# A short-convolution and latent-attention block: the attention and the first part of its output projection put into the hand-written instruction list, and weight parts moved from GpSimd to VectorE

## The chip, the cores and the metric

The kernel runs on one core of a Trainium2 chip. The metric is the device time in microseconds (us). The engines are named as the profile names them: PE is TensorE (matmuls and transposes), DVE is VectorE, ACT is ScalarE, POOL is GpSimd, SP is SyncE, which here only issues DMAs.

## The reference, cut to what matters

One convolution layer and one attention layer, each followed by a gated feed-forward part, on 1024 tokens of width 1024, with 8 heads. All arithmetic is float32. The part that the change touches:

```python
k_nope, v = kv[..., :128], kv[..., 128:]          # kv = c_lat @ w_ukv, per head
q = (cq @ w_uq).reshape(b, s, 8, 128 + 64)
q_pe = apply_rope(q[..., 128:], cos_h, sin_h)     # the last 64 of each head are rotated
# for each block of 128 queries:
sc = einsum('bqhd,bkhd->bhqk', qn_b, k_nope) + einsum('bqhr,bkr->bhqk', qr_b, k_pe)
p = softmax(where(mask, sc * scale, neg))         # causal mask
o = einsum('bhqk,bkhd->bqhd', p, v)
h = h + attn.reshape(b, s, 8 * 128) @ w_o         # the output projection
```

## The kernel before, in words

**Products.** A float32 product is made of three matmuls in the type float32r: each operand is held as a high part and a low part (what is left), and high*high, high*low and low*high are summed. `split` makes the parts: ACT copies to the high part (line 111), then DVE, or another engine if told, subtracts it from the source (line 112). `gemm` (lines 146 to 150) and `three` (lines 153 to 155) issue the matmuls. Activations lie with features on the partitions and 1024 tokens along the free dimension.

**The order of the work.** Most stages are written as one list, a `Steps` object. Each step holds a piece of PE work; functions can be hung before or after a step, to load something, to make parts or to empty a PSUM bank. `run` emits all this in a region in which every engine keeps the order of emission. A step number smaller by two means: emitted two PE pieces earlier. The attention is not such a list. Its functions are called one after the other, and the framework's scheduler sets the order on each engine by its own estimate of time.

**The attention before.** `steps.run()` ends the list of the stages ahead (feed-forward of the first layer, latent products, and the K, Q and V of head 0 and K of head 1, in `ahead`). Then a loop runs over the 8 heads. In each, `scores` (line 1438 its matmuls) makes eight blocks of 128 queries against 128 to 1024 keys: five products, the mask by a minimum (1439), the maximum (1441), its scaling (1442), the exponential with its row sum on ACT (1445), the reciprocal (1446) and the scaling of the block on DVE (1447). `pv` transposes the blocks by PE (1460, tile `ps_t`), splits them (tile `pt`) and multiplies with the values (1469 to 1471, tile `ps_pv`), with the product two key blocks behind the transposes. `pv` for the first four query blocks (g = 0) comes in the same head, for the last four (g = 1) in the next one. Between them stand the jobs that make K, Q, V and the rotated part of Q for the next heads (`make_k`, `make_q`, `make_v`, `make_qr`). Their weights are loaded and split by `Weights.all`, which gives the low part to POOL. `make_qr` also adds and splits on POOL. During head 7 the jobs are `project_o`, the output projection's share of heads 0 to 4 for the eight output blocks; its weights' low parts are on POOL too (`wsplit`). Heads 0 to 5 are stored in DRAM (`od`) and read back, heads 6 and 7 stay in SBUF.

**What comes after.** A second `Steps` list begins with `Plain`, the projection's share of heads 5 to 7 (tile `pl`), whose weights are loaded and split by `wo_load` and `wo_parts`; then the norm and the feed-forward of the second layer.

**Buffers.** PSUM in the attention (`ATT_PS`) has two double banks (tag `ps2`: wide scores, K, Q, V, projection) and four single banks (tag `ps1`: narrow scores, transposes, `ps_pv`). The weights' raw data share five buffers, the parts of the weights four.

## Time and profile before

| | us |
|---|---|
| median of 3 runs (lowest, highest) | 2126.71 (2124.61, 2128.39) |
| the profiled execution | 2122.53 |
| its span, first to last instruction | 2120.6 |
| first scores' matmul, last start of one | 1096.7, 1389.2 |

The profiled execution lies 4.2 us below the median, and 1.9 us of it lie outside the span. In the rows of groups, the name before the arrow is the tile written, those behind it are read; after x stands the count, then the busy time and the mean of one in ns, then the idle time of the engine before them and what ended it. A row of the waits names who waited, what for, the sum in us, how often and the longest. A row of windows gives for each engine its busy time in that stretch and in brackets its instructions, then the granted clock of PE (1.00 is full), the share of the DMA engines and their rate. Matmuls overlap, so the duration of one is longer than the distance to the next.

### The profile page before, as it was taken

How to read it: one execution, taken by the hardware profiler on the slowest of the kernel's cores; microseconds unless marked ns; L12 is line 12 of the kernel's file. 1: busy time of each engine (PE TensorE's matmuls, PEld its weight loads, DVE VectorE, ACT ScalarE, POOL GpSimd, SP SyncE). 2: the span in 40 equal slices, each digit the busy share in tenths (PEclk: the TensorE clock that was granted, in tenths of full speed). 3: DMA queues.
4: the chain of work that ended last, by engine and by line, in shares of the span. 5: the costliest groups of instructions: out<-in, count | busy, mean ns of one | idle time of the engine just before them, and what ended most of it. 6: DMA issues, size and time to landing. Idle time of an engine off the chain costs nothing.

```text
span 2120.6 us, 25572 instructions
## 1 busy us (share of the span) xinstructions
PE 2066.0 (97%) x9542; PEld 1706.4 (80%) x9542; DVE 1460.6 (69%) x2175; ACT 858.0 (40%) x1439; POOL 315.2 (15%) x412
## 2 busy tenths in 40 slices
PE   7999999999999999999999999989999999999998
PEld 6778888888888887787888888877888888888777
DVE  5787656887666668867577777437886666667555
ACT  7423434433333333354245555225433333333445
POOL 2233200122122210000023232101111111100000
PEclk9999999999999999999999999999999999999999
DMA  7255775586766586564232223325487475685543
GB/s 231 70 120 121 226 269 178 117 204 188 186 165 153 139 286 230 193 226 146 70 69 69 65 63 121 138 79 174 128 200 178 149 169 154 154 322 193 179 148 120
DMA packets 274315, 338.96 MB, mean 160 GB/s; under 512 B 18047, under 2 KB 177984, under 8 KB 273872
## 3 DMA queue, kind: packets, MB, share of 16 engines
q1 hardware_dynamic: 240144, 262.71, 38.1%
q0 software_dynamic: 33888, 74.56, 16.4%
q8 instruction: 74, 1.21, 0.2%
q14 instruction: 49, 0.40, 0.1%
q10 hardware_dynamic: 160, 0.07, 0.0%
HBM read 260.22 MB, written 126.35 MB: 182 GB/s over the span
## 4 chain that ended last, share of the span: by engine, by line
PE 83%; DVE 7%; DMA 4%; ACT 3%; issue 2%; SPq 0%; POOL 0%; DVEq 0%; ACTq 0%; POOLq 0%
PE q L154 16%; PE q L153 16%; PE q L155 16%; PE dn L155 4%; PE dn L154 4%; PE dn L153 4%; PE ps_s L1438 4%; PE pl L155 2%; PE pl L153 2%; PE pl L154 2%; DVE wp_lo L112 1%; PE ps_t L1460 1%; PE ps_l L155 1%; PE ps_l L153 1%; PE ps_l L154 1%
## 5 line engine op out<-in xcount | busy, mean ns | idle before, releaser
L153 PE MATMUL q<-xh,w_hi 128*128 128x512 f32 x1568 | 613.3, 391 | 6.3 <-ACT w_hi L111 2.6
L154 PE MATMUL q<-xl,w_hi 128*128 128x512 f32 x1568 | 611.5, 390 | 2.9 <-DVE xl L317 2.9
L155 PE MATMUL q<-xh,w_lo 128*128 128x512 f32 x1568 | 611.5, 390 | 0.9 <-DVE w_lo L112 0.9
L153 PEld LDWEIGHTS q<-xh,w_hi 128*128 128x128 f32 x1568 | 294.8, 188 | 70.6 <-ACT w_hi L111 3.8
L154 PEld LDWEIGHTS q<-xl,w_hi 128*128 128x128 f32 x1568 | 294.7, 188 | 65.9 <-DVE xl L317 4.8
L155 PEld LDWEIGHTS q<-xh,w_lo 128*128 128x128 f32 x1568 | 294.7, 188 | 63.2 <-DVE w_lo L112 2.4
L112 DVE TENSOR_TENSOR w_lo<-wr,w_hi 128x512 fp32r<-128x512 f32 (+1 forms) x272 | 196.6, 723 | 215.1 <-ACT w_hi L111 214.2
L111 ACT CAST w_hi<-wr 128x512 fp32r<-128x512 f32 (+1 forms) x272 | 170.1, 630 | 372.1 <-DVE wr L390 151.2
L155 PE MATMUL dn<-mp_hi,wp_lo 128*128 128x512 f32 (+1 forms) x628 | 245.3, 391 | 6.3 <-DVE wp_lo L112 4.5
L153 PE MATMUL dn<-mp_hi,wp_hi 128*128 128x512 f32 (+1 forms) x628 | 244.3, 389 | 1.0 <-ACT wp_hi L111 1.0
L154 PE MATMUL dn<-mp_lo,wp_hi 128*128 128x512 f32 (+1 forms) x628 | 243.3, 387 | 0.9 <-DVE mp_lo L112 0.9
L1050 POOL COPY paced<-pace 128x1 f32<-128x1 f32 x128 | 84.8, 663 | 923.0 <-ACT pace L1049 923.0
L112 DVE TENSOR_TENSOR mp_lo<-m,mp_hi 128x1024 fp32r<-128x1024 f32 x84 | 95.3, 1134 | 127.2 <-ACT mp_hi L111 125.6
L111 ACT CAST mp_hi<-m 128x1024 fp32r<-128x1024 f32 x84 | 82.2, 979 | 209.8 <-PE dn L154 204.0
L155 PEld LDWEIGHTS dn<-mp_hi,wp_lo 128*128 128x128 f32 x628 | 118.3, 188 | 38.8 <-DVE wp_lo L112 15.5
L153 PEld LDWEIGHTS dn<-mp_hi,wp_hi 128*128 128x128 f32 x628 | 118.3, 188 | 25.5 <-ACT wp_hi L111 2.8
L154 PEld LDWEIGHTS dn<-mp_lo,wp_hi 128*128 128x128 f32 x628 | 118.4, 188 | 25.5 <-DVE mp_lo L112 1.3
L112 DVE TENSOR_TENSOR wp_lo<-w,wp_hi 128x1024 fp32r<-128x1024 f32 x84 | 94.8, 1128 | 0.0
L111 ACT CAST wp_hi<-w 128x1024 fp32r<-128x1024 f32 x84 | 82.0, 976 | 0.0
L1445 ACT ACTIVATE p<-ps_s,mx,rq 128x128 f32<-128x128 f32 (+3 forms) x64 | 53.3, 834 | 56.6 <-DVE mx L1442 51.4
L382 DVE TENSOR_TENSOR w_lo<-wr,w_hi 128x1024 fp32r<-128x1024 f32 x56 | 68.7, 1226 | 7.6 <-ACT w_hi L378 7.6
L738 DVE TENSOR_TENSOR h<-h,dn 128x512 f32<-128x512 f32 x108 | 68.7, 679 | 0.0
(292 smaller groups left out, 3218.8 us busy)
## 6 DMA issues: line engine op xcount, KB each, us to landing
m<-md_f SPq DMA_DIRECT2D x70, 512.0 KB, 4.9
md_f<-c SPq DMA_DIRECT2D x110, 256.0 KB, 3.4
wr<-in_conv_ffn_w_dram SPq DMA_DIRECT2D x47, 512.0 KB, 5.7
wr<-in_mla_ffn_w_dram SPq DMA_DIRECT2D x47, 512.0 KB, 5.4
w<-mw_f SPq DMA_DIRECT2D x40, 512.0 KB, 3.9
h<-hd SPq DMA_DIRECT2D x32, 512.0 KB, 9.3
wr<-in_conv_w_in_dram SPq DMA_DIRECT2D x31, 512.0 KB, 5.2
mw_f<-in_conv_ffn_w_dram POOLq DMA_DIRECT2D x30, 512.0 KB, 7.2
```

What stands on the lines that cost most here:

```text
L111: nc.scalar.copy(out=hi, in_=src)
L112: (eng or nc.vector).tensor_tensor(lo, src, hi.bitcast(F32), ALU.subtract)
L153: nc.tensor.matmul(ps, lhsT=wh, rhs=xh, start=st, stop=False, **more)
L154: nc.tensor.matmul(ps, lhsT=wh, rhs=xl, start=False, stop=False, **more)
L155: nc.tensor.matmul(ps, lhsT=wl, rhs=xh, start=False, stop=en, **more)
L382: nc.vector.tensor_tensor(lo, self.ra, hi.bitcast(F32), ALU.subtract)
L738: nc.vector.tensor_tensor(hv, hv, banks[q], ALU.add if sign > 0 else ALU.subtract)
L1050: nc.gpsimd.tensor_copy(b, a)
L1438: nc.tensor.matmul(ps[:, a:b], lhsT=q[:, qs], rhs=k[:, a:b], start=i == 0, stop=i == 4)
L1445: nc.scalar.activation(p[:, :kw], ps[:, :kw], AF.Exp, bias=mx, scale=rq[:, qb:qb + 1], accum_out=rsum)
L1460: nc.tensor.transpose(t[:, j * P:(j + 1) * P], ps_[j][:, kb * P:(kb + 1) * P], ident)
```

## The change

The attention and the shares of heads 0 to 4 of the projection become steps of the same list as the stages ahead and behind; `steps.run()` between them goes, and with it the second `Steps()`. So every engine takes their instructions in the order written. `scores`, `pv` and `make_qr` are cut into pieces for this. The products stay the same.

- The order of a head: S is the product of one query block (S0 to S7), P the ten or six pieces of `pv`. Odd heads (1, 3, 5): S0 S1 S2 S3, rotated Q, four pieces of the head before's g = 1, Q, the other six, S4 S5, three pieces of g = 0, K, one piece, S6, two pieces, first half of V, S7. Even heads (2, 4, 6): S0 to S3, second half of V, Q, all ten late pieces, S4 S5, three pieces, K, one piece, S6, two pieces, S7. Head 0 has Q for head 1 after S3 and no K; head 7 has output blocks 0, 1 and 2 in the places of the jobs, then 3, 4, five late pieces, 5, five late pieces, 6, 7.
- A block's scaling (reciprocal and scaling) is emitted two steps after its product. For query blocks 4 to 7 the scaling is done by ACT instead of DVE.
- The weights of K, Q and V are loaded nine steps ahead and split four steps ahead, those of the projection six and two; the low parts are made by DVE instead of POOL.
- The rotated part of Q for heads 2 to 7 is made by two ACT copies with the halves of the partitions exchanged, two multiplications 1024 wide, an addition and a split, all on ACT and DVE, spread over seven steps. For the second multiplication a tile `nsin` is loaded (two more DMAs, once).
- `wo_load` and `wo_parts` for heads 5 to 7 stand six steps and one step ahead of `Plain`.

```diff
+        rot["nsin"] = pslot("nsin", "nsin", 1)
+        for q in range(2):
+            nc.sync.dma_start(rot["nsin"][q * 64:q * 64 + 64], rd[1, 64 - q * 64:128 - q * 64])
...
-        def all(self):
-            self.load()
-            return self.split(nc.gpsimd, lo_tile)
...
+    def qr_pieces(h, w):
+        b = {}
+        def product():
+            b["ps"] = q_product(w())
+            b["t"], b["qr"] = tmp("rt"), tmp("qr")
+        def turned(q):
+            nc.scalar.copy(out=b["t"][q * 64:q * 64 + 64], in_=b["ps"][64 - q * 64:128 - q * 64])
+        def cos():
+            nc.vector.tensor_tensor(b["qr"], b["ps"], rot["cos"], ALU.mult)
+        def sin():
+            nc.vector.tensor_tensor(b["t"], b["t"], rot["nsin"], ALU.mult)
+        def add():
+            nc.vector.tensor_tensor(b["qr"], b["qr"], b["t"], ALU.add)
+        def parts():
+            yh, yl = tmp("qrh", dt=F32R), tmp("qrl", dt=F32R)
+            split(yh, yl, b["qr"])
+            qr_moves(h, yh, yl)
+        return product, lambda: turned(0), cos, lambda: turned(1), sin, add, parts
...
+        def scale():
+            p, rsum = Ps[h, qb]
+            nc.vector.reciprocal(rsum, rsum)
+            if qb < 4:
+                nc.vector.tensor_scalar(p[:, :kw], p[:, :kw], rsum, None, ALU.mult)
+            else:
+                nc.scalar.activation(p[:, :kw], p[:, :kw], AF.Copy, scale=rsum)
...
-    steps.run()
...
+    def project_load(n):
+        wo_w[n] = Weights("wo", w_o[:, 0:5, n * P:(n + 1) * P], [P, 5, P])
+        wo_w[n].load()
+        st.h[n] = slot("h")
+        nc.sync.dma_start(st.h[n], hd[n])
...
+    def a_scores(h, *qbs):
+        for qb in qbs:
+            product, scale = scores(h, qb)
+            m = steps.add(product)
+            steps.before(m + 2, scale)
+    def a_job(w, fn):
+        box = {}
+        m = steps.add(lambda: fn(box["w"]))
+        steps.before(m - 9, w.load)
+        steps.before(m - 4, lambda: box.update(w=w.split(new_hi=lo_tile)))
+        return m, box
+    def a_project(n):
+        m = steps.add(lambda: project_o(n))
+        steps.before(m - 6, lambda: project_load(n))
+        steps.before(m - 2, lambda: wo_w.update({n: wo_w[n].split(new_hi=lo_tile)}))
+    def a_rotated(h):
...
+        steps.before(m - 9, w.load)
+        steps.before(m - 4, lambda: box.update(w=w.split(new_hi=lo_tile)))
+        for j, fn in zip((0, 0, 2, 4, 5, 6), pieces):
+            steps.after(m + j, fn)
...
+    for h in range(H):
+        p0 = pv(h, 0)
+        a_scores(h, 0, 1, 2, 3)
+        if h == 7:
+            steps.before(len(steps.pe), lambda: O1.extend([load_o(5, r_(), r_())]))
+            a_project(0)
+            a_steps(late)
+        elif h == 0:
+            a_job(W_q(1), lambda w: make_q(1, w))
+        elif h % 2:
+            a_rotated(h + 1)
+            a_steps(late[:4])
+            a_job(W_q(h + 1), lambda w, h=h: make_q(h + 1, w))
+            a_steps(late[4:])
         else:
+            steps.add(lambda h=h, vbox=vbox: make_v(h, vbox["w"], 1))
+            a_job(W_q(h + 1), lambda w, h=h: make_q(h + 1, w))
+            a_steps(late)
+        a_scores(h, 4, 5)
+        a_steps(p0[:3])
+        if h == 7:
+            a_project(1)
+        elif h:
+            m, _ = a_job(W_k(h + 1), lambda w, h=h: make_k(h + 1, w))
...
+        a_steps(p0[3:4])
+        a_scores(h, 6)
+        a_steps(p0[4:])
+        if h == 7:
+            a_project(2)
+        elif h % 2:
+            _, vbox = a_job(W_v(h + 1), lambda w, h=h: make_v(h + 1, w, 0))
+        a_scores(h, 7)
+        late = pv(h, 1)
+    a_project(3)
+    a_project(4)
+    a_steps(late[:5])
+    a_project(5)
+    a_steps(late[5:])
+    a_project(6)
+    a_project(7)
+    n0 = len(steps.pe)
+    for j, k in enumerate((5, 6, 7)):
+        steps.before(n0 - 6 + j, lambda k=k: wo_load(k))
+        steps.before(n0 - 1 + j, lambda k=k: wo_parts(k))
```

## The prediction

> **What bounds the kernel now.** I read the page first (the engines' shares, then the chain that ended last by engine), then the windows of the attention, then the list of PE's waits there.

> ```profile
> PE 2066.0 (97%) x9542; PEld 1706.4 (80%) x9542; DVE 1460.6 (69%) x2175; ACT 858.0 (40%) x1439; POOL 315.2 (15%) x412
> ...
> PE 83%; DVE 7%; DMA 4%; ACT 3%; issue 2%; SPq 0%; POOL 0%; DVEq 0%; ACTq 0%; POOLq 0%
> ```

> The reader is to see that PE is busy for nearly the whole span and carries the chain. The edit leaves every matmul in place, none more and none fewer. So only PE's waits can move, and in the main only in the stretch that the edit reorders: the heads, from 1080 to 1420 us.

> ```profile
> core 0: us, PE busy (x) PEld busy (x) DVE busy (x) ACT busy (x) POOL busy (x), PEclk, DMA share, GB/s
> 1080.00:1335.00 255.00, 244.32 (x1422) 213.23 (x1421) 193.75 (x458) 132.05 (x274) 72.29 (x101) 1.00 0.31 89
> 1335.00:1420.00 85.00, 77.84 (x367) 64.31 (x364) 31.46 (x49) 20.09 (x35) 9.40 (x6) 0.96 0.27 90
> 1391.40:1394.81 3.41, 0.56 (x4) 0.25 (x2) 3.14 (x4) 1.33 (x2) 0.00 (x0) 1.00 0.91 333
> 1394.81:1401.64 6.83, 6.23 (x15) 4.88 (x16) 2.72 (x5) 1.29 (x2) 0.00 (x0) 0.50 0.70 212
> ...
> PE ps_wo L146 <- DVE h L1521: 3.5, 1, 3.5
> PE ps_s L1438 <- ACT p L1445: 3.4, 2, 2.6
> ```

> PE idles 10.7 us (255.00 - 244.32) in heads 0 to 6 and 7.2 us at the end. There the two long waits leave a window of 3.41 us with 0.56 of PE work, and the next 6.83 us run at clock 0.50, which loses 3.4 more. In all 21.3 us: what an order that never lets PE wait would give back. DVE has 61 us free in the first window and ACT 123, so neither is full; what counts is how long a chain across DVE and ACT is against the PE work put beside it.

> **What is removed, added, moved.** PE's prices, from the timeline:

> ```profile
> 1202.75 0.60 PE L1460 MATMUL ps_t<-ident,p 128*128 128x128 f32 x4
> 1207.58 0.27 PE L1460 MATMUL ps_t<-ident,p 128*128 128x128 f32 x1
> 1208.17 0.63 PE L148 MATMUL ps_k<-lat_part,wk_hi 128*128 128x512 f32 x2
> 1208.64 0.62 PE L150 MATMUL ps_k<-lat_part,wk_lo 128*128 128x512 f32 x2
> ```

> A transpose takes (0.60 - 0.27)/3 = 0.11 us, a 512-column matmul 0.47/2 = 0.23; narrower ones I scale by columns. DVE, then ACT, by shape:

> ```profile
> L112 DVE TENSOR_TENSOR pt<-ps_t,pt 128x512 fp32r<-128x512 f32 x48 | 31.9, 681 | 7.8 <-ACT pt L111 7.7
> L112 DVE TENSOR_TENSOR pt<-ps_t,pt 128x384 fp32r<-128x384 f32 x16 | 8.8, 550 | 0.5 <-ACT pt L111 0.5
> L112 DVE TENSOR_TENSOR pt<-ps_t,pt 128x128 fp32r<-128x128 f32 x16 | 4.5, 283 | 7.2 <-ACT pt L111 7.2
> L112 DVE TENSOR_TENSOR qnl<-ps_q,qnh 128x1024 fp32r<-128x1024 f32 x7 | 8.6, 1222 | 14.0 <-ACT qnh L111 14.0
> L1439 DVE TENSOR_TENSOR ps_s<-ps_s,cmask 128x128 f32<-128x128 f32 x64 | 18.2, 293 | 23.7 <-PE ps_s L1438 23.1
> L1442 DVE TENSOR_SCALAR mx<-mx,nrq 128x1 f32<-128x1 f32 x64 | 12.5, 202 | 0.2
> L1446 DVE RECIPROCAL rsum<-rsum 128x1 f32<-128x1 f32 x64 | 10.0, 156 | 12.3 <-ACT p L1445 12.1
> L1441 DVE TENSOR_REDUCE mx<-ps_s 128x1 f32<-128x1024 f32 x8 | 9.8, 1223 | 0.2
> L1441 DVE TENSOR_REDUCE mx<-ps_s 128x1 f32<-128x896 f32 x8 | 8.7, 1092 | 0.2
> L1441 DVE TENSOR_REDUCE mx<-ps_s 128x1 f32<-128x768 f32 x8 | 7.6, 953 | 0.1
> L1441 DVE TENSOR_REDUCE mx<-ps_s 128x1 f32<-128x512 f32 x8 | 5.5, 685 | 0.0
> L1441 DVE TENSOR_REDUCE mx<-ps_s 128x1 f32<-128x128 f32 x8 | 2.3, 281 | 0.0
> L1447 DVE TENSOR_SCALAR p<-p,rsum 128x1024 f32<-128x1024 f32 x8 | 6.0, 749 | 0.2
> L1447 DVE TENSOR_SCALAR p<-p,rsum 128x512 f32<-128x512 f32 x8 | 4.5, 556 | 0.1
> L1447 DVE TENSOR_SCALAR p<-p,rsum 128x128 f32<-128x128 f32 x8 | 2.2, 278 | 0.1
> ...
> L111 ACT CAST pt<-ps_t 128x512 fp32r<-128x512 f32 x48 | 27.3, 594 | 30.9 <-PE ps_t L1460 29.5 <-DVE mx L1441 1.0
> L1445 ACT ACTIVATE p<-ps_s,mx,rq 128x1024 f32<-128x1024 f32 x8 | 9.7, 1208 | 11.5 <-DVE mx L1442 7.8 <-PE ps_s L1438 3.7
> L1445 ACT ACTIVATE p<-ps_s,mx,rq 128x896 f32<-128x896 f32 x8 | 8.8, 1099 | 18.6 <-DVE mx L1442 18.6
> L1445 ACT ACTIVATE p<-ps_s,mx,rq 128x768 f32<-128x768 f32 x8 | 8.0, 1000 | 1.2 <-DVE mx L1442 1.2
> L111 ACT CAST qnh<-ps_q 128x1024 fp32r<-128x1024 f32 x7 | 7.1, 1010 | 0.0
> L111 ACT CAST wo_hi<-wo_raw 128x640 fp32r<-128x640 f32 x8 | 5.8, 729 | 32.8 <-PE ps_wo L148 20.2 <-issue 12.4 <-DMA wo_raw<-in_mla_w_o_dram 0.2
> L111 ACT CAST wqn_hi<-wqn_raw 128x384 fp32r<-128x384 f32 x6 | 3.1, 519 | 5.2 <-issue 5.1
> ...
> L112 POOL TENSOR_TENSOR wo_lo<-wo_raw,wo_hi 128x640 fp32r<-128x640 f32 x8 | 12.5, 1567 | 65.0 <-ACT wo_hi L111 63.6 <-PE ps_s L1438 1.4
> wo_raw<-in_mla_w_o_dram SPq DMA_DIRECT2D x8, 320.0 KB, 3.0
> ```

> Moved work. The low weight parts leave POOL (1.57 us for 640 columns) for DVE, at its rows of equal width. The scaling of the four wide score blocks (up to 0.75 on DVE) goes to ACT; no row shows that. Its bounds are a cast of that width (0.73 at 640, 1.01 at 1024) and an exponential (1.21 at 1024); I take the cast, the plainer operation. The rotation becomes 1024-wide: on DVE 1.22 each for cos, sin, add and low part, on ACT two half-height copies bounded by zero and 1.01. These totals fit into the free time. The new weight loads on SP stand 6 to 9 steps ahead, over 5 us of PE work against 3.0 to land; the two `nsin` loads precede their use by a head; POOL's queue keeps only its DMAs and gets shorter. I cost these at nothing; the bound on a load that comes late is its landing, 3.0, once.

> What costs is the order. Every engine now takes its instructions as the list emits them. Three places in each head make PE wait; S4 is the scores' product of query block 4 (640 keys), T0 the transposes of key block 0, V0 its product with the values, O0 output block 0 of the projection.

> Place A, after S5. ACT's order is exp of S5, scaling of S4, then the first `pt`. PE has T0 to T2 (9 transposes, 1.0) and then V0, which needs that `pt`. Chain from S5's end: 0.29 + 0.95 + 0.20 + 1.00 + 0.73 + 0.59 = 3.8. PE waits 2.8, and V0's second matmul 0.45 more (DVE's 0.68 less one matmul): 3.2. In heads 1 to 6 the low part of K's weight stands on DVE ahead of S5's minimum and waits for ACT to end S4's exp and the high part: from S4's end 0.29 + 0.8 + 0.20 + 0.9 + 0.2 + 0.4 + 0.4 = 3.2 (values between the rows of the widths beside), against 1.7 of S5: about 1.4 more. Sum: 2 x 3.2 + 6 x 4.6 = 34.

> Place B, where the late transposes begin. Even heads (2, 4, 6): from S7's end DVE does S7 (1.71), S0 to S3 (3.88, four reductions between 0.28 and 0.69), five reciprocals and four scalings (2.56), a weight part 0.55, V's low part and Q's (1.22 each), `pt` 0.68: 11.8. It starts 1.2 late and stands about 3.5 waiting for ACT (2.2 for the exp of S7, its scaling and 0.52 of Q's weight, which stand in that order; 1.3 for V's high part behind the exp of S3): 16.4 with a little overlap between neighbours. PE has S0 to S3 2.9, V 2.8, Q 18 x 0.23 = 4.1, 12 transposes 1.3, one matmul: 11.4. Wait 5.0. Odd heads (1, 3, 5): 11.4 of DVE work (three weight pieces 0.85 and cos 1.22, neither V nor Q), 2.3 late because `ol` of the head before stands on DVE ahead of S7's minimum and waits for `oh`, and that behind the scaling of S6 (0.29 + 1.09 + 0.20 + 1.10 + about 0.9 + 0.59 + 0.68 and the reciprocal, 5.0, against V2, V3 and S7, 2.8 of PE work; for the even heads half of V's product, 2.8, and its low part come between, hence their 1.2), and 1.6 waiting for the exp of S7 and the weight's high pieces: 15.1 against PE's 8.5; 6.5. Head 7: O0's weight stands on ACT behind the exps of S7, S0 and S1 and the scaling of S7 and is there 8.2 after S7's end, PE at 2.9: 5.3; and `pt` stands behind O0's addition to `h` on DVE: 1.2. Sum: 15 + 19.5 + 6.5 = 41.

> Place C, odd heads, after Q: ACT 1.01, DVE 1.22 + 1.22 + 0.68, against T4, V2, T5, V3, T6 and one matmul, 2.6: 1.5; then the rotation's low part 1.22 ahead of the next `pt`: 1.2. Sum: 3 x 2.7 = 8. At the end O2 waits 2.9 for a weight part behind the exp of S6, O4 0.5: 3.4.

> New waits 86.5, less the 21.3 that go: +65. The profiled execution took 2122.5 (span 2120.6), so 2187.7; the median shown is 4.2 above it, and against the median I forecast **2192 us**.

> [...]

> ```profile
> L1447 DVE TENSOR_SCALAR p<-p,rsum 128x256 f32<-128x256 f32 x8 | 4.1, 513 | 0.0
> L1447 DVE TENSOR_SCALAR p<-p,rsum 128x384 f32<-128x384 f32 x8 | 3.3, 412 | 0.0
> ```

> The narrower block takes longer, 0.17 over the 0.35 between its neighbours, as if something held DVE up in some of the eight. That is 8 x 0.17 = 1.4 us of DVE in all, and it stands inside B, so I leave it out. [...]

> **Rivals.**
> Bare chains: DVE and ACT are never late, and only what the order forces is left. A 8 x 2.8 = 22.4; B 1.4, 1.6 and 1.1 (Q's evictions, or cos with two weight steps, or the addition, less 1.53 of transposes and a matmul) = 10; C 8. That is 40 - 21 = +19: 2146. For it: DVE's 61 us free. Against: in B DVE's own list (11.8 and 11.4) is longer than PE's (11.4 and 8.5) even if it never waits.

> Half clock: each A and B leaves PE without products for 4 us or more (the transposes before included), and the window quoted shows what follows 3.41 us with 0.56 of work. Twelve of the fifteen places, 3.41 us at 0.50 each, lose 1.7: +20, so 2212. Against: a window must fall into the gap. [...]

> Faster: the end of head 7 decides. O3 and O4, 60 x 0.23 = 13.6 us, now stand between S7 and its transposes, so the two long waits and the half clock go: 7.2 + 3.4 = 10.6, and 2116. It decides only if heads 0 to 6 wait no longer than their 10.7, 1.5 a head; A alone is 2.8.

> No change: the order is one the engines already had in effect, 2127. Against it: in the timeline before, products of one head stand between another's transposes.

> **How the numbers follow.** Forecast 0.42, bare chains 0.20, half clock 0.27, faster 0.07, no change 0.04. All but the last two are slower: 0.89. The range runs from just under bare chains to half clock with the dearer ends: the scaling at an exponential's price (0.2 in each A and each late start, 3 us) and, as after 1394.81, two half-clock windows instead of one at six places (10 us): 2145 to 2225. It leaves out the last two cases. A measurement tells about 0.2% (4 us) from nothing.

> **What would show it.** Right: waits of `ps_pv` for ACT's `pt` and DVE's `pt` lead PE's list, about 8 of 3 us or more; PE idles some 85 us between 1080 and the first `pl`; POOL computes nothing there. Half clock: digits under 9 in the clock row of those slices. Wrong: if PE idles under 21 us there, A's chain is covered by work that I have not seen.

## The result and the profile after

| | before | after |
|---|---|---|
| median, same chip (us) | 2125.66 | 2241.69 |
| lowest, highest (us) | 2122.12, 2128.39 | 2238.28, 2244.04 |
| ratio of after to before | | 1.0546, 95% interval 1.0524 to 1.0567 |
| profiled execution, its span (us) | 2122.53, 2120.6 | 2238.28, 2235.2 |

The changed kernel is 116 us slower; the prediction said 65 us slower, and its range ended at 2225. The engine shares of the page after, and its clock row:

```profile
PE 2120.3 (95%) x9542; PEld 1739.0 (78%) x9542; DVE 1469.2 (66%) x2170; ACT 892.4 (40%) x1477; POOL 266.7 (12%) x373
...
PEclk9999999999999999999988888889999999999999
```

PE has as many instructions as before (9542), yet it is busy for 54 us more, and seven slices of the clock row show an 8. Where the time lies is told by the first matmul of the stage behind the heads, tile `pl` (last two numbers: first and last start). Before, then after:

```profile
L153 PE MATMUL pl<-oth,wo_h x48: 389/389/791, 1420.2 to 1457.6; 128*128 128x512 f32 x48
```

```profile
L153 PE MATMUL pl<-oth,wo_h x48: 389/389/795, 1534.2 to 1572.4; 128*128 128x512 f32 x48
```

It starts 114.0 us later, so nearly all of the loss lies in the heads. Windows of after: the heads, then the surroundings of place A of head 1.

```profile
1080.00:1534.20 454.20, 375.70 (x1779) 310.26 (x1780) 230.10 (x499) 187.21 (x348) 34.85 (x68) 0.87 0.22 64
...
1158.29:1161.70 3.41, 0.00 (x0) 0.00 (x0) 1.85 (x5) 1.47 (x3) 0.00 (x0) 1.00 0.14 38
1161.70:1168.53 6.83, 5.97 (x13) 4.41 (x14) 1.65 (x4) 2.38 (x5) 0.00 (x0) 0.50 0.00 0
```

PE idles 78.5 us there (454.20 - 375.70), 60.7 more than the 17.8 of before. It is busy 53.5 us more than before's 322.2 (244.32 + 77.84) with the same work. That second half is the clock: its mean is 0.87, so about 2 x 0.13 x 454 = 118 us ran at half speed, called the half clock here (119.5 us in 22 stretches by the clock's own records). The two lower rows show one of them: a window without PE work, then 6.83 us at 0.50. PE's waits, and the instructions at that place (a row of the timeline gives the start, the duration, the engine, line, operation and tiles, the count, and in brackets how long the engine had idled and what ended it):

```profile
PE ps_pv L1513 <- ACT pt L111: 42.7, 14, 4.4
PE ps_pv L1514 <- DVE pt L112: 17.6, 14, 1.7
PE ps_wo L146 <- ACT wo_hi L111: 7.8, 3, 4.3
PE ps_q L146 <- ACT wqr_hi L111: 5.6, 3, 1.9
PE ps_s L1472 <- DVE ol L112: 1.6, 3, 0.5
```

```profile
1157.00 1.15 PE L1501 MATMUL ps_t<-ident,p 128*128 128x128 f32 x9
...
1158.26 0.42 DVE L112 TENSOR_TENSOR wk_lo<-wk_raw,wk_hi 128x256 fp32r<-128x256 f32 x1 [1.40 <-ACT wk_hi L111]
1158.61 0.29 DVE L1473 TENSOR_TENSOR ps_s<-ps_s,cmask 128x128 f32<-128x128 f32 x1
1158.93 0.96 DVE L1475 TENSOR_REDUCE mx<-ps_s 128x1 f32<-128x768 f32 x1
...
1160.23 0.99 ACT L1479 ACTIVATE p<-ps_s,mx,rq 128x768 f32<-128x768 f32 x1 [2.00 <-DVE rsum L1484]
...
1161.22 0.82 ACT L1488 ACTIVATE p<-p,rsum 128x640 f32<-128x640 f32 x1
1161.93 0.57 ACT L111 CAST pt<-ps_t 128x512 fp32r<-128x512 f32 x1
...
1162.56 0.80 PE L1513 MATMUL ps_pv<-pt,vh 128*128 128x512 f32 x1 [4.42 <-ACT pt L111]
```

This is place A as predicted: the nine transposes are done, and V0 stands still until ACT has ended the exp of S5 (768 wide), the scaling of S4 and the first `pt`. K's low part stands ahead of S5's minimum on DVE, and DVE has idled 1.40 us for `wk_hi` before it.

### The profile page after: what moved, and what is told of

Its sections match the earlier page's. It is cut to its first block, busy times and chain, and to the rows that moved or that the text cites. A ratio compares the mean times of both kernels' runs of the same rounds, so it can differ in the third digit from the quotient of the medians.

```text
span 2235.2 us, 25547 instructions
## 1 busy us (share of the span) xinstructions
PE 2120.3 (95%) x9542; PEld 1739.0 (78%) x9542; DVE 1469.2 (66%) x2170; ACT 892.4 (40%) x1477; POOL 266.7 (12%) x373
## 3 DMA queue, kind: packets, MB, share of 16 engines
q8 instruction: 74, 1.21, 0.2%
## 5 line engine op out<-in xcount | busy, mean ns | idle before, releaser
L155 PEld LDWEIGHTS q<-xh,w_lo 128*128 128x128 f32 x1568 | 294.7, 188 | 63.6 <-DVE w_lo L112 2.6
L112 DVE TENSOR_TENSOR w_lo<-wr,w_hi 128x512 fp32r<-128x512 f32 (+1 forms) x272 | 196.6, 723 | 214.9 <-ACT w_hi L111 214.0
L111 ACT CAST w_hi<-wr 128x512 fp32r<-128x512 f32 (+1 forms) x272 | 170.1, 630 | 370.7 <-DVE wr L390 151.0
L112 DVE TENSOR_TENSOR mp_lo<-m,mp_hi 128x1024 fp32r<-128x1024 f32 x84 | 95.2, 1134 | 127.7 <-ACT mp_hi L111 126.0
L111 ACT CAST mp_hi<-m 128x1024 fp32r<-128x1024 f32 x84 | 82.2, 979 | 210.2 <-PE dn L154 204.5
L112 DVE TENSOR_TENSOR wp_lo<-w,wp_hi 128x1024 fp32r<-128x1024 f32 x84 | 94.8, 1128 | 0.0
L1513 PE MATMUL ps_pv<-pt,vh 128*128 128x512 f32 (+1 forms) x96 | 43.8, 457 | 42.7 <-ACT pt L111 42.7
L111 ACT CAST wp_hi<-w 128x1024 fp32r<-128x1024 f32 x84 | 82.0, 976 | 0.0
L112 DVE TENSOR_TENSOR pt<-ps_t,pt 128x512 fp32r<-128x512 f32 (+1 forms) x96 | 50.4, 552 | 47.1 <-ACT pt L111 47.1
```

The source lines that it names most:

```text
L111: nc.scalar.copy(out=hi, in_=src)
L112: (eng or nc.vector).tensor_tensor(lo, src, hi.bitcast(F32), ALU.subtract)
L155: nc.tensor.matmul(ps, lhsT=wl, rhs=xh, start=False, stop=en, **more)
L1513: nc.tensor.matmul(o[:, c], lhsT=vh, rhs=th, start=kb == 0, stop=False)
```

## The experiments

The kernel before had medians of 2123.00, 2123.45 and 2123.39 us beside the first four, the next four and the last four. PE's idle time is that of the windows from 1080 us to the first `pl`, "half clock" the time that the clock's records show at half speed there.

| run | us | ratio, 95% interval | PE idle in the heads | half clock |
|---|---|---|---|---|
| before | 2126.71, 2125.66 | | 17.8 | 6.8 |
| after | 2241.69 | 1.0524 to 1.0567 | 78.5 | 119.5 |
| 1 free order | 2114.36 | 0.9939 to 0.9973 | 8.5 | 6.8 |
| 2 before, off POOL | 2130.00 | 1.0017 to 1.0043 | 20.8 | 10.2 |
| 3 PE kept busy | 2200.74 | 1.0349 to 1.0380 | 12.8 | 0.0 |
| 4 low parts on POOL | 2209.28 | 1.0387 to 1.0418 | 62.2 | 75.1 |
| 5 only PE by hand | 2138.14 | 1.0050 to 1.0094 | 25.6 | 13.7 |
| 6 only DVE and ACT by hand | 2210.97 | 1.0398 to 1.0433 | 67.8 | 78.5 |
| 7 K first | 2228.69 | 1.0482 to 1.0520 | 76.2 | 85.3 |
| 8 free order, POOL | 2108.40 | 0.9911 to 0.9955 | 6.0 | 0.0 |
| 9 busy with matmuls | 2211.37 | 1.0388 to 1.0432 | 30.5 | 23.9 |
| 10 busy with transposes | 2213.78 | 1.0399 to 1.0441 | 34.3 | 27.3 |
| 11 scaling on DVE | 2215.11 | 1.0411 to 1.0458 | 70.8 | 75.1 |
| 12 as 8, scaling on DVE | 2108.77 | 0.9908 to 0.9946 | 5.8 | 0.0 |

### 1, 5, 6: whose order is it

The heads' steps are emitted in the same sequence in all three, but only the named engines must keep it.

```diff
 # the stretch of the list from the first to the last step of the heads
-with tc.manual_schedule():
+with ExitStack():                                                    # 1
+with tc.manual_schedule(engines={mybir.EngineType.PE}):              # 5
+with tc.manual_schedule(engines={mybir.EngineType.DVE, mybir.EngineType.Activation}):  # 6
```

> The changed kernel with its heads emitted in the same sequence, but outside the ordered region, so that the framework's scheduler sets the order on each engine, as before. Theory (the order written by hand on the engines makes PE wait, and the waits bring half clock): the time returns to 2115 to 2140 us, PE's idle time in the heads to about 20 us, half clock to under 15 us. Rival (the moved work, off POOL and onto DVE and ACT, is what costs): stays above 2200 us, since the instructions are the same.

> The changed kernel with only PE's order by hand in the heads; DVE, ACT, POOL and SP in the scheduler's order. Theory (the order on ACT and DVE is what makes PE wait: the first pt needs nothing of S5's softmax, it only stands behind it): most of the gain of the free order, 2114 to 2140 us, waits of ps_pv for pt under 15 us. Rival (the order of PE's own pieces leaves too little between a block and its transposes): above 2190 us.

> The changed kernel with only DVE's and ACT's order by hand in the heads; PE's by the scheduler. Theory: the chains on DVE and ACT stay as long as they are, and PE can only pull some products ahead into the gaps: 2150 to 2210 us. Rival (PE's order is what costs): under 2130 us.

With nobody bound the same list is 8.6 us faster than before; with PE alone bound it is 14.7 slower, with DVE and ACT alone 87.5, with all of them 116. So it is in the main the order on DVE and ACT that costs: 96 us over the free list, where PE's order alone costs 23. Run 5's waits of `ps_pv` for `pt` are 22.2 us together, above the 15 expected; run 6 ends at the upper edge of what was expected for it. The timeline of run 1 near S4 of head 1 shows what the scheduler does otherwise:

```profile
1142.07 0.48 ACT L111 CAST pt<-ps_t 128x384 fp32r<-128x384 f32 x1 [0.19 <-PE ps_t L1503]
...
1142.44 0.90 ACT L1481 ACTIVATE p<-ps_s,mx,rq 128x640 f32<-128x640 f32 x1
...
1143.32 0.37 ACT L111 CAST pt<-ps_t 128x256 fp32r<-128x256 f32 x1
1143.48 0.72 PE L146 MATMUL ps_k<-lat_part,wk_hi 128*128 128x512 f32 x2
...
1145.12 1.65 ACT L1490 ACTIVATE p<-p,rsum 128x640 f32<-128x640 f32 x2
```

These two `pt` still belong to the last pieces of head 0. The scheduler has put the products of S4 and S5 ahead of those pieces, so that S4's exp runs between the `pt` and its scaling behind them, while PE does K's product. The transposes of head 1's g = 0 start later in this trace, at 1147.53, their first product at 1153.14, with S6 and much of V's product between them; PE does not wait there, although the scaling stands ahead of their `pt` on ACT here too. In runs 5 and 6 the waits are short and many, or long and of another kind. PE's longest rows of 5, then of 6:

```profile
PE ps_pv L1516 <- DVE pt L112: 15.3, 24, 2.1
PE ps_pv L1515 <- ACT pt L111: 6.9, 13, 1.0
```

```profile
PE ps_k L146 <- ACT wk_hi L111: 22.7, 6, 3.8
PE ps_s L1474 <- DVE vl L112: 9.1, 4, 2.7
```

With PE bound and the others free no wait is over 2.2 us. With DVE and ACT bound PE goes round most of place A (`pt` on ACT falls from 14 waits to 2, one of them 6.2 us) and runs into the next: `wk_hi` on ACT, six times.

### 2: the other part alone

The kernel before, with the low parts of the weights and the rotated Q's addition and split on DVE.

```diff
-        split(hi[:, :n], lo[:, :n], raw[:, :n], eng=nc.gpsimd)
+        split(hi[:, :n], lo[:, :n], raw[:, :n], eng=nc.vector)
...
-            return self.split(nc.gpsimd, lo_tile)
+            return self.split(nc.vector, lo_tile)
...
-def make_qr(h, w=None, new=lambda: ps2("ps_q"), eng=nc.gpsimd):
+def make_qr(h, w=None, new=lambda: ps2("ps_q"), eng=nc.vector):
```

> The kernel before with one part of the change alone: the low weight parts, and the rotated Q's addition and split, on DVE instead of POOL; no order by hand. Theory: within 8 us of the kernel before, 2118 to 2134. Rival (DVE becomes too full): slower by 30 us or more.

7 us slower: taking work off POOL is a small loss here, not the 116.

### 3, 9, 10: what the half clock costs

The changed kernel, with matmuls by a tile of zeros on PE at most places where it would wait, 323 in all (the text on record ahead of the run says about 420): 5 to 18 ahead of V0 in most heads, 2 to 7 ahead of its second matmul, 8 ahead of the rotated Q, up to 18 ahead of O0 to O2, a few in place C. They add zeros. Run 9 keeps only those ahead of a product's first matmul; run 10 has two transposes of the zero tile in place of each.

```diff
+still["t"] = pslot("still", "still", 1, F32R, [P, P])
+nc.vector.tensor_tensor(still["t"], ident, ident, ALU.subtract)
...
+nc.tensor.matmul(o, lhsT=still["t"], rhs=rhs, start=first, stop=False)      # 3, 9
+nc.tensor.transpose(o[:, i % 4 * P:i % 4 * P + P], still["t"], ident)       # 10
```

> The changed kernel with about 420 more matmuls with zero weights, put where PE waits and sized a little under each wait, so that PE is not idle; the work and its order on the other engines stay. Theory (the waits are set by DVE and ACT, about 60 us, and half clock costs some 54 us on top): half clock nearly gone, time falls by 45 to 55 us, to 2187 to 2197. Rival (half clock only falls into waits and costs little by itself; without it PE waits longer): 2230 to 2250 as the changed kernel.

> The changed kernel with matmuls by zero weights only where TensorE stands still ahead of the first matmul of a product (before V0's first, in the late heads, before the rotated Q's product, before O0, O1 and O2), none between the two matmuls of one product. It is the reference point of the next run. Theory (half clock follows an idle stretch of some 3 us, and matmuls that do nothing keep it away): the long stillstands of place A are covered, so the half clock in the heads falls from 119.5 us to under 40 us, and the time to 2200 to 2220 (the run with fillers everywhere gave 2200.7). Rival (the half clock follows the sum of many short waits, not one stretch): the half clock stays over 80 us and the time at 2230 or more.

> The same places as the run before it, filled with transposes on TensorE in place of matmuls, two for one; their output is overwritten by the product that follows. [...] Theory B (any instruction on TensorE's array counts): half clock under 40 us and 2200 to 2225, as with the matmuls.

The heads of run 3:

```profile
1080.00:1496.10 416.10, 403.35 (x2108) 333.15 (x2109) 231.10 (x501) 187.48 (x348) 34.81 (x68) 1.00 0.24 71
```

The clock is full, and the time falls by 41 us although PE has more to do. The stretch is still 75.9 us longer than before's 340.2: that is what the waits alone cost (with an estimated 0.23 at most at a place, the distance of two matmuls of 512 columns, where a matmul by zeros is still running when the wait ends). So of the 116 the half clock is about 40: 41 between the two medians, 38 when each run is taken against the kernel before measured beside it (116.0 and 77.7 us slower). That is a little under the 45 to 55 expected. PE was busy 53.5 us longer by it; that the missing 12 to 15 had lain beside work of DVE and ACT, for which PE would have waited anyway, fits these numbers but was not measured by itself.

Run 9 is 10.6 us above run 3: the short waits that it leaves, of 0.5 to 2 us and most of them inside a product, also bring the half clock (23.9 us of it). Runs 9 and 10 agree (2211.37 and 2213.78 us, half clock 23.9 and 27.3), and run 10 lies where theory B had it. Its windows just after place A's beginning in head 1, and the only group of PE in the first of them:

```profile
1159.72:1163.13 3.41, 3.41 (x33) 3.35 (x31) 1.62 (x5) 1.69 (x3) 0.00 (x0) 1.00 0.15 41
1163.13:1166.54 3.41, 2.72 (x12) 1.87 (x11) 1.37 (x4) 2.16 (x5) 0.00 (x0) 1.00 0.00 0
```

```profile
L1467 PE MATMUL ps_pv<-ident,still 128*128 128x128 f32 x33 | 3.8, 272 | 0.0
```

A stretch of 3.41 us holds nothing but transposes, and the next one runs at 1.00. A stretch without PE work at the same place in after was followed by 0.50. So the transposes of this kernel, which the trace lists as MATMUL, held the full clock as the matmuls by zeros did: 27.3 us of half clock against 23.9. Whether transposes alone bring PE back from half clock, no run here shows.

### 4, 7, 11: shortening the waits under the order by hand

Each is the changed kernel with one edit: the weights' low parts back on POOL (4), K's product ahead of the first pieces of `pv` in heads 1 to 6 (7), the wide scaling back on DVE (11).

```diff
-w.split(new_hi=lo_tile)
+w.split(nc.gpsimd, lo_tile)                       # 4
-        a_steps(p0[:3])                           # 7: behind K's product
-            if qb < 4:
+            if qb < 8:                            # 11
```

> The changed kernel with the low parts of the weights back on POOL, order by hand kept. Theory: DVE no longer stands before the maximum of S5 for K's weight, so the wait before the first product of g = 0 falls in heads 1 to 6 from 4.6 to the 3.2 us of heads 0 and 7, and the waits at the late transposes by about 1 us in odd and even heads: 10 to 15 us less waiting, with half clock 10 to 25 us less time, 2217 to 2232. Rival (the move off POOL is the main cause): under 2150.

> The changed kernel with K's product ahead of the first three pieces of g = 0 in heads 1 to 6; all else in its order. Theory: the wait behind S5 falls in six heads from 5.1 to about 1.8 us (K's product covers it, but pt now stands behind K's eviction): 20 us less waiting and 10 to 20 less of half clock, 2200 to 2212 us. Rival (DVE and ACT are simply full, and the wait comes back elsewhere): 2230 to 2242.

> The changed kernel, order by hand, with the wide scaling of the early scores back on VectorE instead of ScalarE. Theory (place A is the chain of exp and scaling that stand one behind the other on ScalarE, 4.58 us in heads 1 to 6): the scaling leaves that chain, place A falls by the 0.7 us by which the scaling holds up the exp, 5 to 9 us of waits in all, and with the half clock that goes with them the time is 2225 to 2240. Rival (place A is set by VectorE, which has the weights' low parts and the additions): the scaling comes later on VectorE than it did on ScalarE, place A grows, and the time is 2245 to 2270.

Run 4's two first waits, against 42.7 and 17.6 of after:

```profile
PE ps_pv L1513 <- ACT pt L111: 28.7, 14, 3.0
PE ps_pv L1514 <- DVE pt L112: 15.0, 15, 1.5
```

The longest wait falls from 4.4 to 3.0: the 1.4 us that the prediction gave to K's low part on DVE. From start to start, the wait of V0's first matmul falls from 4.58 to 3.18 in heads 1 to 6. PE idles 16.3 us less, and the time falls by 32, more than the 10 to 25 expected: the half clock falls from 119.5 to 75.1 us with the waits, and PE is busy 15.4 us less with the same work.

Run 7 missed: 2228.69 lies between the theory and the rival. K's product does cover part of A, but now it waits itself for the exp of S4, in a row that after does not have (S4 and S5 hold the two double banks that K's product would use):

```profile
PE ps_k L146 <- ACT p L1479: 5.0, 6, 0.8
```

And `pt` stands behind K's eviction and the scaling of S5 on ACT. PE idles 76.2 us, hardly less than 78.5; most of the 13 us gained lie in the half clock (85.3 against 119.5 us).

In run 11 the waits fall by 7.7 us, inside the 5 to 9 expected, but the time by 26.6, to under the 2225 to 2240 expected: the half clock falls from 119.5 to 75.1 us. In heads 1 to 6 the wait of V0's first matmul falls to 3.2 to 3.9 us, and even heads have 0.65 instead of 2.33 at the late transposes; odd heads have 3.31 instead of 1.38 there. The rival was wrong on place A, which did not grow; a scaling that comes late on DVE shows only in place B of the odd heads.

### 8, 12: a version that beats both

Run 1 with the low parts on POOL (8), and that with the scaling on DVE (12); the edits are those of runs 4 and 11.

> The free order (heads outside the ordered region) with the low parts of the weights back on POOL. If off-POOL costs in a free order what it cost in the kernel before (about 7 us, 0.3%, with the rotation's share in it), this gains 3 to 7 us on the free order: 2107 to 2112 us, faster than both kernels. Rival (with the wide scaling on ACT, DVE has room and POOL's slower parts come late): 2114 to 2120.

> The emission free to be reordered, the weights' low parts on GpSimd (the run that gave 2108.4), and the wide scaling on VectorE instead of ScalarE: what is left of the change's own edits in the heads is then next to nothing. Theory (the gain over the kernel before comes from the tail, O3 and O4 between the last scores and the transposes, not from the scaling on ScalarE): 2106 to 2113. Rival (the gain comes from the scaling on ScalarE): 2115 to 2126.

Both are 15 us faster than before (0.7%), and the scaling's engine makes no difference. Windows of run 12; the second is the end of the heads:

```profile
1080.00:1320.00 240.00, 235.25 (x1372) 205.74 (x1370) 188.12 (x424) 129.71 (x264) 58.49 (x93) 1.00 0.30 82
1320.00:1404.40 84.40, 83.33 (x423) 70.32 (x424) 40.88 (x79) 27.38 (x52) 11.16 (x9) 1.00 0.40 129
```

At the end PE idles 1.1 us where before idled 7.2 and lost 3.4 to the clock; ahead of it 4.75 against 10.7. Together 15.4 us, against 14.6 measured. With the weights and the scaling back on their engines, what is left of the change is the sequence of emission (O3 and O4 between S7 and its transposes among it), the earlier loads and the rotated Q on ACT and DVE; these weren't tried apart. The prediction's third rival, that the end of head 7 gives back 10.6, fits the sequence emitted freely (9.5 of the 15.4 lie there) and is false of the order by hand.

## Why the prediction was wrong

**What bounds the kernel: right.** PE, with the same instructions; the whole loss is PE standing still or running at half speed in the heads.

**The waits: right in sum, nearly right in place.** Taken from start to start in the timeline after, less the usual distance of two matmuls, 0.11 us for transposes and 0.23 for 512 columns (A and B hold the wait of the first matmul and that of the second):

| place | predicted | measured |
|---|---|---|
| A, heads 0 and 7 | 3.2 | 3.68 |
| A, heads 1 to 6 | 4.6 | 5.08 |
| B, even heads | 5.0 | 4.29 |
| B, odd heads | 6.5 | 5.76 |
| head 7, O0 and `pt` | 5.3 + 1.2 | 5.15 + 1.16 |
| C, odd heads | 2.7 | 2.91 |
| O2, O4, and O1 | 3.4 | 4.64 |
| sum | 86.5 | 87.7 |

That the sum is so close is in part luck: A is 3.8 us dearer in all, B with head 7 4.5 cheaper. Net of what goes, PE idles 60.7 us more, where the prediction had 68.6 (86.5 less 10.7 and 7.2). Run 3, with the half clock gone, gives +77.7 (2200.74 - 2123.00) against the 65 predicted. Two steps were off. In the odd heads 2.7 of the 5.76 are not at the late transposes but ahead of them: S3 waits 0.7 for `ol` on DVE (the row of 1.6 us above), and the rotated Q's product 2.03 for `wqr_hi`, which stands on ACT behind exps (the row of 5.6 us); the prediction had let PE run through both and counted a single wait behind them. And the scaling on ACT was taken at a cast's price. Groups of after:

```profile
L1488 ACT ACTIVATE p<-p,rsum 128x1024 f32<-128x1024 f32 x8 | 9.1, 1142 | 4.9 <-DVE rsum L1484 4.9
...
L1488 ACT ACTIVATE p<-p,rsum 128x640 f32<-128x640 f32 x8 | 6.5, 816 | 0.0
```

It took 0.82 at 640 and 1.14 at 1024, over the cast's 0.73 and 1.01 and nearer to the exponential's end of the bounds (1.21 at 1024).

**The half clock: the step that failed.** The prediction left it out of the sum and made it a rival at 20 us: twelve places, one window of 3.41 each, 1.7 lost in each. Measured, it is about 40 us. All three factors were low. Places: 22, since the odd heads go to half clock three times each (behind `wqr_hi`, B and C), at waits of 1.2 to 2.0 us. Length: 13 of the 22 stretches last 6.83 us, among them all eight of place A; only the upper end of the range had reckoned with two windows, at six places. Condition: "a window must fall into the gap" was the argument against it, and the windows ahead of half clock were not all empty: PE was busy for up to 55% of them, as below. The forecast took "PE waits" and "PE runs slowly" for two cases to choose between. They come together: waits of that size brought the half clock with them, and the sum should have held both. Against the kernels before measured beside them, the 116.0 us are the 65 predicted, 12.7 by which the waits of run 3 lie above it (77.7), and 38.3 of half clock. The forecast's own signs were met (waits of `ps_pv` for `pt` lead PE's list, PE idles 78.5 us, POOL computes nothing), and the sign of the half clock was met beside them.

**The rivals.** Bare chains (2146) is out: DVE and ACT were late as worked out. No change is out: run 1 emits the same sequence, and binding it changes 127 us. Faster is out for this kernel; run 12 is 14.6 us faster than before, but which part of its sequence does it was not tried.

**Something held DVE up in some of the eight: right.** The block of 256 columns that took longer than its neighbours, after and in run 2:

```profile
L1486 DVE TENSOR_SCALAR p<-p,rsum 128x256 f32<-128x256 f32 x8 | 2.8, 353 | 0.3
```

```profile
L1447 DVE TENSOR_SCALAR p<-p,rsum 128x256 f32<-128x256 f32 x8 | 2.8, 345 | 0.0
```

From 513 ns it falls to 345 to 353 where POOL makes no low parts (350 in run 5, 353 in run 6), and with them back it takes 391, 464 and 603 (runs 4, 8, 12). The trace of before shows it one by one. Two of the eight took 1.03 us: they began while POOL made the low part of the rotated Q, and ended 0.15 us behind it; the other six took 0.33 to 0.35, with no subtraction or addition of POOL beside them. A block of 384 columns that began 0.16 us ahead of an addition on POOL took 0.41, as its neighbours did. By what way the subtraction holds DVE up, no run shows. In the kernel before it is worth 8 x 0.16 = 1.3 us of DVE in this row, and taking POOL's work away does not pay: runs 8 and 12, with POOL, are the fastest.

## What to carry to other kernels

An order written out by hand binds every engine, and here it cost most on those that only serve: one exp, one scaling and one copy in the wrong order on ACT stop PE for 3.2 us in every head, and a weight part on DVE for 1.4 more in six of them, while the same list used as a mere sequence of emission was faster than before. Bind one engine at a time and measure each. When waits that add up to over about 1.5 us within 3.4 us are foreseen on PE (each of the 22 windows ahead of half clock in after had that much), price the half clock with them: here 60.7 us more of idle came with 53.5 us more of busy PE, and removing 7.7 us of waits (run 11) gave 26.6.

## What the runs showed of the hardware

```profile
1124.20:1127.60 3.40, 1.53 (x7) 0.93 (x6) 1.75 (x6) 1.88 (x5) 0.09 (x1) 0.99 0.49 150
1127.60:1131.00 3.40, 3.40 (x9) 2.65 (x8) 3.12 (x14) 2.42 (x6) 0.00 (x0) 0.51 0.28 80
1148.00:1151.40 3.40, 1.58 (x6) 0.92 (x7) 2.89 (x6) 1.86 (x4) 1.52 (x4) 1.00 0.20 39
1151.40:1154.80 3.40, 3.40 (x16) 3.40 (x16) 0.87 (x2) 0.58 (x1) 3.09 (x7) 0.51 0.91 217
```

PE is busy for 1.53 and 1.58 of 3.40 us, 45% and 46%, and the next window is at half speed. Cut into the windows of that grid, the heads of after part cleanly: the 22 windows at full clock that were followed by half clock had PE busy for at most 55%, the 75 followed by full clock for at least 59%. Once at half clock, the 13 windows that were followed by another had PE busy for at most 86%, the 22 that ended it for all of the window. The two windows at half clock in before agree: PE busy for 2.82 of 3.42 us (82%) in the one that was followed by another, for all 3.41 in the one that ended it. Elsewhere windows at full clock with less work kept it: three of before with PE busy for 55%, and 3.41 us of run 11 (from 1198.70) with 1.47 busy, 43%, after which the clock was 1.00. So the bound is about half and not sharp in these records. This fits the 6.83 us of place A: the window in which PE starts again holds the rest of the wait (5.97 busy of the two together in the rows of head 1, all of what is missing in the first), and a second one follows at half clock.
